# Negated queries and masks: the masked row minimum as the bias of the exponentials

## The chip, the cores and the metric

The kernel runs on one core of one Trainium2 chip. The metric is the device time of one execution in microseconds, as the median over several executions.

## The reference

One layer of a decoder trunk on a sequence of 2048 positions with 1024 features, in float32. The input is normalised and projected; of the projection 512 columns go to eight attention heads of 64 and 2 x 512 columns to a gated linear recurrence (RG-LRU with a short convolution). Both results are joined by an output projection, and a squared-ReLU MLP of width 4096 follows, each with norms and residual.

The attention is a mixture of three dilated sliding windows (window 128 with dilation 1, 512 with 4, 2048 with 16). For each branch:

```python
s = einsum('bchnqd,bchnkd->bchnqk', qb, kb) * (HEAD_DIM ** -0.5)
s = where(valid, s, -inf)
mx = max(s, axis=-1, keepdims=True)
p = exp(s - mx)
den = sum(p, axis=-1)
o = einsum('bchnqk,bchnkd->bchnqd', p, vb) / den[..., None]
lse = mx[..., 0] + log(den)
```

The branches' outputs are then weighted by the softmax over their `lse`.

## The kernel before

All products run as three passes over operands that are split in a high and a low part (`split`, L52: ACT casts the high part at L54, DVE or POOL subtracts it at L55). The sequence is worked in two halves of 1024 positions (`hf` 0 and 1).

First the input projection of both halves runs, with the recurrence and the attention of the first half among it. The order of these steps is the string `ORDER` (L1557), in which `a0` to `a3` are the attention of four pairs of heads, `q..` projections of queries, keys and values (`Project.qkv`, L203) and `r..` blocks of the recurrence (`recurrent_block`, L296). In this part the order of the instructions on each engine is chosen by the framework's scheduler from a simulated timeline (`schedule_with_timeline_sim`, L1610).

Then the first half goes through output projection, MLP input (`mlp_in`) and MLP output (`mlp_out`). PE's order is written by hand from here on. The attention of the second half is interleaved with the first half's `mlp_out` by `interleave` (L1299); in this block ACT, DVE and SP run in the written order too (L1538). `interleave` takes one step of `mlp_out` after another (a product of three matmuls, L1140 to L1142, and a part of the split of a later factor, L1223 on ACT and L1225 on DVE), and puts the parts of an attention unit between them. The exponentials of a unit are issued behind the first of these steps. The second half's projections and MLP follow.

The attention has two parts for each head. Part A (`part_a`, L501) handles the window of dilation 1: per step two blocks of 128 queries against 256 keys each, in one PSUM bank. Part B (`part_b`, L561) covers the other two windows, merged through a mask that holds the logarithm of how often a key counts: per step 384 or 512 keys in the second half, 128 and 256 together in the first. A unit is one (head, block) of part A or one (head, residue) of part B. For each:

- PE writes the scores into PSUM (L529 for A, L586 and L587 for B).
- `softmax_rows` (L400): for each block DVE adds the mask, writes the masked scores to `sm` and their row maximum to one column of the statistics tile `st[:, 0]` (L404: a custom instruction and a read of its accumulator). Then one DVE instruction writes the negated maxima of the step to `neg` (L411). `exps` (L413) has ACT take exp(sm + neg) in place, with the row sums to `st[:, 1]` (L415). In the first half `exps` is called at once; in the second it is returned to `interleave`.
- PE transposes the probabilities (L377), ACT and DVE split them (`thA`, `tlA`, `thB`, `tlB`; L54, L55), PE multiplies them by the values (L553, L612), and `fold` (L394) adds the halves.

`join` (L630) brings the maxima and sums of both parts together: PE lays them out (L644, L646), DVE forms the larger maximum and the differences (L651 to L654), ACT their exponentials (L655, L656), and DVE the weights.

The scale of the scores is in the queries: `qkv` multiplies by 1/8 while it applies the norm (L225). The masks are made on the host by `_constants` (L1567), with 0, a logarithm, or -1e30.

Of the kernel before, what the change touches and what calls it, by code (L numbers as in the profile page):

```python
# [8 lines left out]
F32 = mybir.dt.float32  # L9
F32R = mybir.dt.float32r  # L10
AF = mybir.ActivationFunctionType
ALU = mybir.AluOpType
# [3 lines left out]
P = 128  # L16
# [5 lines left out]
HD = 64  # L22
# [12 lines left out]
NEG = -1.0e30  # L35


def f32(ap):
    return ap.bitcast(F32)
# [12 lines left out]
def split(nc, hi, lo, src, lo_eng=None):  # L52

    return (nc.scalar.copy(out=hi, in_=src),  # L54
            (lo_eng or nc.vector).tensor_tensor(out=lo, in0=src, in1=f32(hi), op=ALU.subtract))  # L55
# [31 lines left out]
class Project:  # L87
# [115 lines left out]
    def qkv(self, hf, pr):  # L203

        nc, p, scr = self.nc, self.p, self.scr
        v, pe = nc.vector, nc.tensor
        last = hf == 0 and pr == NP - 1
        steps = [(k, b) for k in range(3) for b in range(NBH)]
        if last:

            steps = [(0, 0), (0, 1), (1, 0), (2, 0), (1, 1), (2, 1)]
        elif hf and pr == FIRST:

            steps = [(0, 0), (1, 0), (0, 1), (1, 1), (2, 0), (2, 1)]
        ws = {}
        for kind, b in steps:
                ct = 4 * kind + pr
                if kind not in ws:
                    ws[kind] = self.load_w(hf, ct)
                w = ws[kind]  # L220
                cs = slice(b * TB, (b + 1) * TB)
                z = self.product(hf, ct, w, b)
                zn = self.pa.tile([P, TB], F32, tag="t512", bufs=3, name=f"zn{hf}_{ct}_{b}")
                if kind == 0:
                    v.scalar_tensor_tensor(out=zn, in0=z, scalar=HD ** -0.5, in1=self.bc[b], op0=ALU.mult,  # L225
                                           op1=ALU.mult)
                else:
                    v.tensor_tensor(out=zn, in0=z, in1=self.bc[b], op=ALU.mult)
                if kind < 2:
                    zh = self.pa.tile([P, TB], F32R, tag="zh", bufs=1, name=f"zh{hf}_{ct}_{b}")  # L230
                    zl = self.pa.tile([P, TB], F32R, tag="zl", bufs=1, name=f"zl{hf}_{ct}_{b}")
                    self.cst["pool"] = split(nc, zh, zl, zn, lo_eng=self.lo)[1]
                    dst = scr["q" if kind == 0 else "k"][hf][pr]
                    for u in range(2):
                        nc.sync.dma_start(out=f32(dst[u, 0, :, cs]), in_=f32(zh[u * HD:(u + 1) * HD, :]))
                        nc.sync.dma_start(out=f32(dst[u, 1, :, cs]), in_=f32(zl[u * HD:(u + 1) * HD, :]))
                else:
                    pt = self.bank("X", f"vt{hf}_{ct}_{b}")
                    for j in range(TB // P):
                        pe.transpose(pt[:, j * P:(j + 1) * P], zn[:, j * P:(j + 1) * P], self.cst["ident"])  # L240
                    ptv = pt.rearrange("p (n h c) -> p n h c", h=2, c=HD)
                    vs = self.pa.tile([P, TB // P, 2, 2, HD], F32R, tag="vst", bufs=1, name=f"vs{hf}_{ct}_{b}")
                    split(nc, vs[:, :, :, 0, :], vs[:, :, :, 1, :], ptv)
                    nc.sync.dma_start(out=f32(scr["v"][hf][pr][cs, :].rearrange("(n p) c -> p n c", p=P)),
                                      in_=f32(vs.rearrange("p n u a c -> p n (u a c)")))
# [106 lines left out]
def attention(tc, p, bank, cst, scr, hf, mask_a_d, mask_b_d, pj, pw=None, px=None):  # L352
# [7 lines left out]
    v, s, g, pe = nc.vector, nc.scalar, nc.gpsimd, nc.tensor  # L360
# [3 lines left out]
    mask_a = p.tile([P, 2 * P], F32, tag="mask_a", name=f"mask_a{hf}")  # L364
    nc.sync.dma_start(out=mask_a, in_=mask_a_d)
    mask_b = p.tile([P, NX * P], F32, tag="mask_b", name=f"mask_b{hf}")
# [32 lines left out]

    def softmax_rows(st, u, cols, sp, sm, parts, mask, name):  # L400

        neg = p.tile([P, len(parts)], F32, tag="neg", bufs=4, name=f"neg{name}")
        for j, (c0, w) in enumerate(parts):
            v.tensor_tensor_reduce(out=sm[:, c0:c0 + w], in0=sp[:, c0:c0 + w], in1=mask[:, mask.shape[-1] - w:],  # L404
                                   scale=1.0, scalar=-3.0e38, op0=ALU.add, op1=ALU.max,
                                   accum_out=st[:, 0, u, cols[j]:cols[j] + 1])
        if len(parts) == 2 and cols[1] != cols[0] + 1:
            mx = st[:, 0, u, cols[0]:cols[1] + 1:cols[1] - cols[0]]
        else:
            mx = st[:, 0, u, cols[0]:cols[0] + len(parts)]  # L410
        v.tensor_scalar(out=neg, in0=mx, scalar1=-1.0, scalar2=None, op0=ALU.mult)  # L411

        def exps(parts=list(parts)):  # L413
            for j, (c0, w) in enumerate(parts):
                s.activation(out=sm[:, c0:c0 + w], in_=sm[:, c0:c0 + w], func=AF.Exp, bias=neg[:, j:j + 1],  # L415
                             accum_out=st[:, 1, u, cols[j]:cols[j] + 1])

        if hf:
            return exps
        exps()  # L420
# [54 lines left out]
    def units(pr):  # L475
# [25 lines left out]
        def part_a(u, b):  # L501
# [5 lines left out]
            def scores(b2):  # L507
                qs, kh, kl, vb, qa = get()
                ka = runs(kh), runs(kl)
                n0 = 4 * b + 2 * b2  # L510
                sp = bank("S", f"S{n_}_{n0}")
                sm = p.tile([P, TB], F32, tag="sm", bufs=SMB[hf], name=f"sm{n_}_{n0}")
                parts = []
                for j in range(2):
                    n = hf * NQH + n0 + j
                    q = qa[:, (n0 + j) * P:(n0 + j + 1) * P]
                    i, r = divmod(n, 4)
                    w = (2 if n else 1) * P
                    c0 = 2 * P * (j + 1) - w
                    parts.append((c0, w))  # L520
                    dst = sp[:, c0:c0 + w].rearrange("p (n c m) -> p n c m", c=NC, m=MR)
                    for x, t in enumerate((kh, kl)):
                        if r:
                            keys = ka[x][:, i, r - 1:r + 1]
                        elif n:
                            keys = across(t, i)
                        else:
                            keys = ka[x][:, 0, 0:1]
                        pe.matmul(dst, q, keys, start=(x == 0), stop=(x == 1))  # L529
                loc[b2] = sm, parts[0][0]  # L530
                return softmax_rows(env["st"]["A"], u, (n0, n0 + 1), sp, sm, parts, mask_a, f"{n_}_{n0}")
# [93 lines left out]
        def ending():  # L625
            return join(pr, env["st"], env["na"], env["nb"])
# [3 lines left out]
    def join(pr, st, na, nb):  # L630
# [5 lines left out]
        for k, sa in enumerate(sas):  # L636
            v.tensor_tensor(
                out=sa, in1=cst["sel"][:, 0:NC].unsqueeze(1).unsqueeze(1).to_broadcast([P, 4, 4, NC]), op=ALU.mult,
                in0=st["A"][:, k].rearrange("p u (i n) -> p n (u i)", n=4).unsqueeze(3).to_broadcast([P, 4, 4, NC]))
# [8 lines left out]
        mA, dA, mB, dB = [pst[0:R, i * P:(i + 1) * P] for i in range(4)]  # L648
        jt = pj.tile([P, TB], F32, tag="jt", bufs=1, name=f"jt{hf}_{pr}")
        gm, eA, eB, dd = [jt[0:R, i * P:(i + 1) * P] for i in range(4)]  # L650
        v.tensor_copy(out=dd, in_=mA)  # L651
        v.tensor_tensor(out=gm, in0=mB, in1=dd, op=ALU.max)
        v.tensor_tensor(out=eA, in0=dd, in1=gm, op=ALU.subtract)
        v.tensor_tensor(out=eB, in0=mB, in1=gm, op=ALU.subtract)  # L654
        s.activation(out=eA, in_=eA, func=AF.Exp)  # L655
        s.activation(out=eB, in_=eB, func=AF.Exp)  # L656
        yield
        v.tensor_tensor(out=dd, in0=dA, in1=eA, op=ALU.mult)
        v.tensor_tensor(out=gm, in0=dB, in1=eB, op=ALU.mult)
# [907 lines left out]
def _constants():  # L1567
    run = np.arange(P).reshape(MR, NC).T.reshape(-1)
    dist = run[:, None] + P - np.concatenate([run, run + P])[None, :]
    mask_a = np.where((dist >= 0) & (dist <= P), 0.0, NEG).astype(np.float32)  # L1570
    dist = np.arange(P)[:, None] + 3 * P - np.arange(4 * P)[None, :]
    mult = ((dist >= 0) & (dist <= P)) * 1 + ((dist >= 0) & (dist % 4 == 0))
    mask_b = np.where(mult > 0, np.log(np.maximum(mult, 1)), NEG).astype(np.float32)
    i = np.arange(P)[:, None]
    sel = np.concatenate([i // MR == np.arange(NC), i % MR == np.arange(MR)], axis=1).astype(np.float32)
    return np.eye(P, dtype=np.float32), sel, mask_a, mask_b
# [37 lines left out]
```

## Time and profile before

| | |
|---|---|
| median of 3 runs | 2313.2 us (2310.83 to 2317.4) |
| the profiled execution | 2311.64 us |
| its span, first to last instruction | 2309.9 us |
| PE busy | 2184.8 us (95%) |
| DVE busy | 1539.9 us (67%) |
| ACT busy | 1231.3 us (53%) |
| POOL busy | 465.9 us (20%) |
| mean share of the DMA engines, 100 to 560 us and 1100 to 1531 us | 0.57 and 0.72 |

PE is TensorE (matmuls), PEld its weight loads, DVE VectorE, ACT ScalarE, POOL GpSimd, SP the engine that issues most DMAs. Matmuls are pipelined and their ends are modelled, so a busy PE is not PE at its peak. Idle time of an engine that is not the bottleneck costs nothing by itself. The chain of waits follows the last instruction back, at each step to what released it or to the instruction before it on its engine; "issue" is time in which the engine waited for nothing that the profile shows. Names such as `sm`, `smB`, `stA`, `neg` are the program's tiles.

### The profile page before, as it was taken

How to read it: one execution, taken by the hardware profiler on the slowest of the kernel's cores; microseconds unless marked ns; L12 is line 12 of the kernel's file. 1: busy time of each engine (PE TensorE's matmuls, PEld its weight loads, DVE VectorE, ACT ScalarE, POOL GpSimd, SP SyncE). 2: the span in 40 equal slices, each digit the busy share in tenths (PEclk: the TensorE clock that was granted, in tenths of full speed). 3: DMA queues.
4: the chain of work that ended last, by engine and by line, in shares of the span. 5: the costliest groups of instructions: out<-in, count | busy, mean ns of one | idle time of the engine just before them, and what ended most of it. 6: DMA issues, size and time to landing. Idle time of an engine off the chain costs nothing.

```text
span 2309.9 us, 30833 instructions
## 1 busy us (share of the span) xinstructions
PE 2184.8 (95%) x10264; PEld 1776.1 (77%) x10264; DVE 1539.9 (67%) x3060; ACT 1231.3 (53%) x2489; POOL 465.9 (20%) x549
## 2 busy tenths in 40 slices
PE   8989989889999899998999999889999999999998
PEld 6668778667788677786777787667878888788887
DVE  6757575887548877674667677767775656545556
ACT  7646464645334555453656666745454545563542
POOL 5543514563213201011001011113200000000003
PEclk9999999999999999999999999999999999999999
DMA  8364574645754586867777777768454433576665
GB/s 288 99 194 154 166 232 146 180 144 151 255 166 155 195 306 255 302 232 268 248 201 211 220 227 204 220 189 257 147 194 169 164 137 155 208 271 195 192 192 182
DMA packets 217553, 466.16 MB, mean 202 GB/s; under 512 B 22465, under 2 KB 77153, under 8 KB 211121
## 3 DMA queue, kind: packets, MB, share of 16 engines
q1 hardware_dynamic: 188624, 329.52, 45.7%
q0 software_dynamic: 28768, 134.66, 16.5%
q8 instruction: 81, 1.33, 0.2%
q14 instruction: 80, 0.65, 0.1%
HBM read 329.75 MB, written 151.13 MB: 208 GB/s over the span
## 4 chain that ended last, share of the span: by engine, by line
PE 59%; DVE 14%; DMA 9%; ACT 7%; issue 5%; POOL 1%; SPq 0%; DVEq 0%; ACTq 0%; POOLq 0%
PE o L1141 6%; PE o L1140 6%; PE o L1142 6%; PE za L1001 4%; PE za L1002 4%; PE za L1003 4%; PE z L198 3%; PE z L199 3%; PE z L200 3%; PE m L827 2%; PE m L825 2%; PE m L826 2%; PE zc L1001 2%; PE zc L1002 2%; PE zc L1003 2%
## 5 line engine op out<-in xcount | busy, mean ns | idle before, releaser
L198 PE MATMUL z<-hH,wH 128*128 128x512 f32 x640 | 263.6, 412 | 17.6 <-ACT wH L54 7.9
L199 PE MATMUL z<-hL,wH 128*128 128x512 f32 x640 | 259.1, 405 | 0.5 <-DVE hL L173 0.5
L200 PE MATMUL z<-hH,wL 128*128 128x512 f32 x640 | 257.9, 404 | 0.0
L198 PEld LDWEIGHTS z<-hH,wH 128*128 128x128 f32 x640 | 122.6, 192 | 51.2 <-ACT wH L54 8.8
L199 PEld LDWEIGHTS z<-hL,wH 128*128 128x128 f32 x640 | 122.3, 191 | 32.0 <-issue 5.1
L200 PEld LDWEIGHTS z<-hH,wL 128*128 128x128 f32 x640 | 122.5, 191 | 28.5 <-issue 3.4
L415 ACT ACTIVATE smB<-smB,negB 128x128 f32<-128x128 f32 (+3 forms) x128 | 71.4, 559 | 103.0 <-DVE negB L411 102.7
L55 POOL TENSOR_TENSOR wL<-wraw,wH 128x512 fp32r<-128x512 f32 x58 | 84.2, 1464 | 115.7 <-ACT wH L54 109.0
L1006 ACT ACTIVATE sq<-sq 128x512 f32<-128x512 f32 x93 | 58.8, 632 | 84.9 <-DVE sq L1010 84.9
L1066 POOL DMA_DIRECT2D sa<-sq x31 | 16.5, 533 | 402.4 <-ACT sq L1007 401.8
L415 ACT ACTIVATE sm<-sm,neg 128x256 f32<-128x256 f32 (+1 forms) x128 | 63.1, 494 | 55.7 <-DVE neg L411 55.2
L55 DVE TENSOR_TENSOR tlB<-pT_B,thB 128x384 fp32r<-128x384 f32 x96 | 57.4, 598 | 44.2 <-ACT thB L54 41.0
L1007 ACT ACTIVATE sq<-sq 128x512 f32<-128x512 f32 x124 | 76.6, 629 | 2.2
L54 ACT CAST wH<-wraw 128x512 fp32r<-128x512 f32 (+1 forms) x81 | 47.2, 612 | 49.5 <-PE z L199 31.7
L1174 POOL TENSOR_TENSOR y<-y,g4b 128x512 f32<-128x512 f32 x8 | 13.0, 1655 | 261.3 <-ACT junk_y L84 261.3
L1077 DVE TENSOR_TENSOR w2s<-w2s 128x512 f32<-128x512 f32 x64 | 44.1, 689 | 32.1 <-DMA w2s<-in_dram 31.2
L404 DVE CUSTOM_DVE_ANT_0 smB<-SB,mask_b 128x128 f32<-128x128 f32 (+3 forms) x128 | 59.5, 482 | 6.8 <-PE pT_B L377 4.2
L377 PE MATMUL pT_B<-ident,smB 128*128 128x128 f32 x320 | 52.7, 280 | 5.3 <-DVE nb L398 2.2
L54 ACT CAST thB<-pT_B 128x384 fp32r<-128x384 f32 x96 | 48.4, 506 | 16.3 <-PE oB L612 14.2
L55 DVE TENSOR_TENSOR tlA<-pT,thA 128x512 fp32r<-128x512 f32 (+1 forms) x64 | 42.5, 668 | 21.0 <-ACT thA L54 20.7
L1001 PE MATMUL za<-hHT,f_6H 128*128 128x512 f32 x128 | 50.6, 396 | 5.2 <-ACT sq L1040 5.1
L1002 PE MATMUL za<-hLT,f_5H 128*128 128x512 f32 x128 | 51.0, 399 | 4.4 <-DVE hLT L55 4.4
(568 smaller groups left out, 7105.7 us busy)
## 6 DMA issues: line engine op xcount, KB each, us to landing
sa<-as POOLq DMA_DIRECT2D x32, 1024.0 KB, 6.5
w1r<-in_dram SPq DMA_DIRECT2D x58, 512.0 KB, 3.8
sa<-sq POOLq DMA_DIRECT2D x31, 768.0 KB, 3.9
wraw<-in_dram SPq DMA_DIRECT2D x79, 256.0 KB, 3.5
w2s<-in_dram SPq DMA_DIRECT2D x16, 1024.0 KB, 7.5
sb<-w2s POOLq DMA_DIRECT2D x16, 1024.0 KB, 6.2
kh<-sk SPq DMA_DIRECT2D x24, 512.0 KB, 5.2
kl<-sk SPq DMA_DIRECT2D x24, 512.0 KB, 6.8
```

Source lines behind the costliest of these rows:

```text
L54: return (nc.scalar.copy(out=hi, in_=src), (lo_eng or nc.vector).tensor_tensor(out=lo, in0=src, in1=f32(hi), op=ALU.subtract))
L55: (lo_eng or nc.vector).tensor_tensor(out=lo, in0=src, in1=f32(hi), op=ALU.subtract))
L198: pe.matmul(z, hi[:, k, :], hh, start=(k == 0), stop=False)
L199: pe.matmul(z, hi[:, k, :], hl, start=False, stop=False)
L200: pe.matmul(z, lo[:, k, :], hh, start=False, stop=(k == KT - 1))
L415: s.activation(out=sm[:, c0:c0 + w], in_=sm[:, c0:c0 + w], func=AF.Exp, bias=neg[:, j:j + 1], accum_out=st[:, 1, u, cols[j]:cols[j] + 1])
L1001: pe.matmul(o, hi[:, k], bh[:, k], start=start and k == 0, stop=False, skip_group_check=True)
L1002: pe.matmul(o, hi[:, k], bl[:, k], start=False, stop=False, skip_group_check=True)
L1003: pe.matmul(o, lo[:, k], bh[:, k], start=False, stop=k == KH - 1, skip_group_check=True)
L1140: pe.matmul(o, ah[:, ts], bh, start=fresh and j == 0, stop=False, skip_group_check=True)
L1141: pe.matmul(o, ah[:, ts], bl, start=False, stop=False, skip_group_check=True)
L1142: pe.matmul(o, al[:, ts], bh, start=False, stop=j == NJ - 1, skip_group_check=True)
```

## The change

The queries are multiplied by -1/8 in place of 1/8, and both masks change sign, so that the masked scores have the opposite sign. The reduction takes their minimum, which is the negative of the former maximum, and stands in `st[:, 0]`. The exponentials have a scale of -1 and take their bias from that column directly; the tile `neg` and the DVE instruction that wrote it are gone. `join` compares by minimum and takes exponentials with a scale of -1.

```diff
@@ qkv
-                    v.scalar_tensor_tensor(out=zn, in0=z, scalar=HD ** -0.5, in1=self.bc[b], op0=ALU.mult,
+                    v.scalar_tensor_tensor(out=zn, in0=z, scalar=-(HD ** -0.5), in1=self.bc[b], op0=ALU.mult,
                                            op1=ALU.mult)
@@ softmax_rows
-        neg = p.tile([P, len(parts)], F32, tag="neg", bufs=4, name=f"neg{name}")
         for j, (c0, w) in enumerate(parts):
             v.tensor_tensor_reduce(out=sm[:, c0:c0 + w], in0=sp[:, c0:c0 + w], in1=mask[:, mask.shape[-1] - w:],
-                                   scale=1.0, scalar=-3.0e38, op0=ALU.add, op1=ALU.max,
+                                   scale=1.0, scalar=3.0e38, op0=ALU.add, op1=ALU.min,
                                    accum_out=st[:, 0, u, cols[j]:cols[j] + 1])
-        if len(parts) == 2 and cols[1] != cols[0] + 1:
-            mx = st[:, 0, u, cols[0]:cols[1] + 1:cols[1] - cols[0]]
-        else:
-            mx = st[:, 0, u, cols[0]:cols[0] + len(parts)]
-        v.tensor_scalar(out=neg, in0=mx, scalar1=-1.0, scalar2=None, op0=ALU.mult)
-
-        def exps(parts=list(parts)):
+
+        def exps(parts=list(parts), cols=list(cols)):
             for j, (c0, w) in enumerate(parts):
-                s.activation(out=sm[:, c0:c0 + w], in_=sm[:, c0:c0 + w], func=AF.Exp, bias=neg[:, j:j + 1],
+                s.activation(out=sm[:, c0:c0 + w], in_=sm[:, c0:c0 + w], func=AF.Exp, scale=-1.0,
+                             bias=st[:, 0, u, cols[j]:cols[j] + 1],
                              accum_out=st[:, 1, u, cols[j]:cols[j] + 1])
@@ join
-        v.tensor_tensor(out=gm, in0=mB, in1=dd, op=ALU.max)
+        v.tensor_tensor(out=gm, in0=mB, in1=dd, op=ALU.min)
         v.tensor_tensor(out=eA, in0=dd, in1=gm, op=ALU.subtract)
         v.tensor_tensor(out=eB, in0=mB, in1=gm, op=ALU.subtract)
-        s.activation(out=eA, in_=eA, func=AF.Exp)
-        s.activation(out=eB, in_=eB, func=AF.Exp)
+        s.activation(out=eA, in_=eA, func=AF.Exp, scale=-1.0)
+        s.activation(out=eB, in_=eB, func=AF.Exp, scale=-1.0)
@@ _constants
-    mask_a = np.where((dist >= 0) & (dist <= P), 0.0, NEG).astype(np.float32)
+    mask_a = -np.where((dist >= 0) & (dist <= P), 0.0, NEG).astype(np.float32)
-    mask_b = np.where(mult > 0, np.log(np.maximum(mult, 1)), NEG).astype(np.float32)
+    mask_b = -np.where(mult > 0, np.log(np.maximum(mult, 1)), NEG).astype(np.float32)
```

## Rows read from the trace of the kernel before

**Rows 1.** Busy time by stretch: us, then each engine's busy us (instructions), clock, DMA, GB/s

```profile
100.00:560.00 460.00, 421.08 (x2115) 338.23 (x2116) 323.41 (x716) 249.71 (x552) 196.75 (x189) 0.96 0.57 172
...
1100.00:1531.00 431.00, 404.81 (x2206) 336.53 (x2204) 308.17 (x766) 274.77 (x617) 37.84 (x68) 1.00 0.72 211
```

**Rows 2.** Groups by form, 1100 to 1531 us: busy us, mean ns | idle before, releaser

```profile
L404 DVE CUSTOM_DVE_ANT_0 sm<-S,mask_a 128x256 f32<-128x256 f32 x64 | 24.3, 416 | 0.1
L415 ACT ACTIVATE smB<-smB,negB 128x512 f32<-128x512 f32 x32 | 23.2, 725 | 42.2 <-DVE negB L411 41.9
...
L411 DVE TENSOR_SCALAR negB<-stB 128x1 f32<-128x1 f32 x64 | 9.8, 154 | 2.2
...
L411 DVE TENSOR_SCALAR neg<-stA 128x2 f32<-128x2 f32 x32 | 5.4, 169 | 1.1
```

**Rows 3.** Waits, 1100 to 1531 us: us in total, times, longest

```profile
ACT smB L415 <- DVE negB L411: 78.2, 54, 3.7
...
ACT sm L415 <- DVE neg L411: 38.8, 27, 2.1
```

**Rows 4.** Chain of waits, 1100 to 1531 us: start us, us, what

```profile
1176.98 0.16 DVE negB L411
...
1263.55 0.34 DVE sm L404
...
1263.93 0.18 DVE neg L411
...
1264.13 1.09 ACT sm L415 x3
...
1519.41 0.04 DVE negB L411
```

**Rows 5.** Busy time by stretch of the second stage, columns as in rows 1

```profile
1123.00:1172.00 49.00, 49.00 (x278) 42.33 (x277) 34.61 (x90) 32.31 (x75) 0.00 (x0) 1.00 0.63 194
1198.00:1230.00 32.00, 29.55 (x177) 24.46 (x177) 23.13 (x64) 22.29 (x53) 0.90 (x2) 1.00 0.51 154
1246.00:1283.00 37.00, 35.65 (x196) 29.81 (x195) 27.24 (x69) 23.42 (x56) 1.12 (x2) 1.00 0.69 220
1303.00:1330.00 27.00, 24.47 (x148) 19.95 (x146) 18.23 (x52) 16.59 (x41) 0.00 (x0) 1.00 0.53 163
1345.00:1386.00 41.00, 40.70 (x225) 34.45 (x223) 30.59 (x77) 28.05 (x65) 1.12 (x2) 1.00 0.73 234
1403.00:1435.00 32.00, 29.28 (x175) 24.30 (x176) 22.74 (x65) 20.31 (x49) 0.46 (x1) 1.00 0.50 160
1435.00:1474.00 39.00, 32.34 (x151) 24.75 (x149) 31.48 (x75) 32.08 (x57) 9.24 (x16) 0.96 0.88 243
1474.00:1531.00 57.00, 55.44 (x303) 46.43 (x303) 41.72 (x99) 34.37 (x79) 2.54 (x4) 1.00 0.53 158
```

**Rows 6.** Groups by form, 100 to 560 us, columns as in rows 2

```profile
L411 DVE TENSOR_SCALAR negB<-stB 128x2 f32<-128x2 f32 x32 | 10.5, 328 | 0.2
...
L318 ACT ACTIVATE r<-pr,vec_br 128x512 f32<-128x512 f32 x13 | 8.8, 681 | 15.9 <-PE pr L313 9.6 <-DVE xc L331 6.3
...
L411 DVE TENSOR_SCALAR neg<-stA 128x2 f32<-128x2 f32 x32 | 7.6, 248 | 0.1
```

**Rows 7.** Chain of waits, 100 to 560 us, columns as in rows 4

```profile
140.85 0.07 DVE neg L411
...
211.06 1.10 DVE neg L411
...
449.15 0.98 DVE negB L411
...
540.89 0.09 DVE negB L411
```

**Rows 8.** PE's waits, 100 to 560 us, columns as in rows 3

```profile
PE pi L315 <- ACT r L318: 7.7, 2, 4.8
PE oA L553 <- DVE state L332: 5.5, 1, 5.5
```

## The prediction

> **What bounds the kernel now.** I first cut the span into stages and read each engine's busy time there. The negations exist in two stages only: 100 to 560 us (attention of the first half of the sequence, among projections and recurrence) and 1100 to 1531 us (attention of the second half, interleaved with the second MLP product). In both PE is busiest: 421 of 460 us and 405 of 431 us; DVE has 323 and 308, ACT 250 and 275 [rows 1]. So PE idles 39 and 26 us there, and what takes work off DVE or ACT can give back little more than that.
>
> Then I read, in the second stage, the groups of instructions by form and the waits. A unit of attention goes in one ring: PE writes scores, DVE adds the mask and takes the row maximum (L404), DVE negates it (L411), ACT takes the exponentials with that as bias (L415), PE transposes, ACT and DVE split the transposes, PE multiplies by the values. 96 negations take 15.2 us there [rows 2], and ACT sat idle until one of them came in 81 cases for 117 us [rows 3]. That idle time is no gain in itself: most of it is ACT having nothing to do.
>
> What counts is the chain that ended last. Walked through this stage in pieces of 20 us, the chain of waits holds a negation 49 times, 19 of the kind of part A (two columns) and 30 of part B (one column); the first, the last and one whole passage of part A are shown [rows 4]. Behind a first reduction the passage reads: second reduction 0.34, negation 0.18, then both exponentials, 1.09 us. Between 1246 and 1283, for instance, the chain is such passages one behind the other, and PE only follows; between 1123 and 1172 PE is never idle, 49.00 of 49 us, and no negation lies on the chain [rows 5]. So the stage changes between PE setting the pace and the DVE-ACT ring setting it.
>
> **The change part by part.** *160 negations go*: 64 in the first stage (18.1 us, because there they take 248 and 328 ns each on average [rows 6]) and 96 in the second.
>
> *Second stage.* Here the orders of ACT, DVE, SP and PE are written out by hand, so nothing else moves. On the chain a part-B negation costs 0.16 plus about 0.02 of issue, 0.18. A part-A one costs 0.18 plus 0.02, 0.20; and since each exponential now needs its own reduction only, the first exponential can start before the second reduction of 0.34 us. The second exponential then waits for its own reduction, but that ends 0.34 us after the first one, while the first exponential takes 0.5 us, so the new wait is over before it is reached and what is queued behind it on ACT (the other exponential, then the casts of the MLP factors) isn't held. A part-A passage is thus worth 0.54. Sum: 30 x 0.18 + 19 x 0.54 = 15.7 us.
>
> That is an upper bound, since PE becomes the pace once the ring is shorter. I cap each stretch by PE's idle time in it [rows 5]: 1198 to 1230, 2.16 wanted (3 A, 3 B), 2.45 idle; 1246 to 1283, 3.06 wanted (4 A, 5 B), 1.35 idle; 1303 to 1330, 1.98 (3 A, 2 B), 2.53 idle; 1345 to 1386, 3.06 (4 A, 5 B), 0.30 idle; 1403 to 1435, 2.16 (3 A, 3 B), 2.72 idle; 1435 to 1474, 0.72 (4 B), 6.66 idle; 1474 to 1531, 2.34 (2 A, 7 B), 1.56 idle. One more B negation at 1177 adds 0.18. With the smaller of each pair the sum is 2.16 + 1.35 + 1.98 + 0.30 + 2.16 + 0.72 + 1.56 + 0.18 = 10.4; I take 10.
>
> Idle time of PE may be too strict a cap, because matmul times overlap. In the stretch without a stall the weight loads are busy 42.33 of 49 us, 86%; between 1246 and 1283 they are at 29.81 of 37, 81% [rows 5]. The Trainium skill ("Perfetto Trace Analysis", section "Identifying the Most-Contended Engine") says that matmul busy time is no good measure of how near PE is to its limit, and that the busy share of the weight loads is. By that, with 86% as full, the caps would be 3.7, 2.5, 3.9, 1.1, 3.9, 10.4 and 3.3 us, and the sum for the stage 13 in place of 10.
>
> *First stage.* The chain holds 13 negations there, 3.15 us together; the first, the last and the two long ones are shown [rows 7]. The long ones (1.10 and 0.98 against some 0.17) are a stall of DVE that its next instruction may inherit, so without them I count 3.15 - 2.08 + 0.34 = 1.4; the earlier first exponential adds up to 8 x 0.34 = 2.7, since 8 of the 13 are of part A. That makes 1.4 to 5.9 if the orders stay. They need not stay: in this stage the queues' orders come from the scheduler's simulated timeline, and 64 instructions fewer on DVE shift it. One operation that lands behind the wrong neighbour has shown what it costs: PE waited 5.5 us once for DVE's state copy (L332) and 4.8 us at the longest for a tanh of ACT (L318) [rows 8]. So the bounds for this stage run from a loss of some 15 us (three such stalls more) to a gain of 8 (5.9 and part of a stall that goes). I take a gain of 2, near what the rows on the chain give.
>
> *At nothing:* the sign in the query's scale (L225) and in the masks, which only changes a constant. The exponentials get a scale of -1 in place of 1; a tanh with a scale and a pointer bias takes 681 ns for 512 columns [rows 6] where the exponential of 512 without a scale takes 725 [rows 2], so a scale costs nothing. The reduction by minimum: nothing shows it, I take the 416 ns of the maximum [rows 2]; it could be shorter or longer, and a tenth either way on the 24.3 us of part A in the second stage is 2.4 us. In the join (L652 to L656) only signs change, 8 times. The stages between, 560 to 1100 and after 1531, hold no negation; they move earlier as a whole.
>
> Sum: 10 + 2 = 12 us against the profiled execution's 2311.6, so 2299.6. The median of the runs shown lies 1.6 above that execution, so I predict 2301.
>
> **The rivals.** *PE or the loads cover it* (27 in 100). After each saving PE or the next load comes last, and only stretches with more idle time than wanted pay: half of the 10.4, and nothing in the first stage, about 5 us; 2308. For it: PE is busy 94% of this stage, and two stretches have 1.35 and 0.30 us idle where 3 are wanted. Against it: in four stretches the idle time exceeds what is wanted [rows 5]. The Trainium skill's page named above says to optimize the most contended engine first, and by busy time that is PE, not DVE; this rival is what that rule gives.
>
> *Slower: the first stage's order is drawn anew* (13 in 100). Place: 100 to 560 us. Four more stalls of the mean of 5.5 and 4.8 us cost 20.6; with the 12 gained that is 8.6 us slower, 2322. It decides from a loss of 19 us on, below that the second stage pays for it. For it: this stage already holds 39 us of PE's idle time, made of such single waits. Against it: PE's idle time can also shrink by the same draw, and DVE has 18 us less to do.
>
> *It does not do what it says* (2 in 100): the exponentials and the next reductions share a tile, and if the framework ordered them by tile, each reduction would wait for an exponential of 0.5 us; ten on the chain are 5 us, sixty 30, slower. Against it: ACT writes its sums into that tile already, and DVE idled 0.1 us before all 64 reductions of part A in the second stage [rows 2].
>
> **How the numbers follow.** A measurement can tell some 0.3% here, 7 us: faster means under 2306, slower over 2320. The forecast keeps 58 in 100, the covered case 27, the two slower ones 15 together. The range takes the uncapped 15.7 with the first stage's best 8 at its low end (24 gained, 2289), and at its high end the forecast's 10 with three stalls more (15.4 lost, 2318), which leaves out the slower rivals and a little below.
>
> **What would show it.** Right: no L411; ACT's idle time before L415 now ends on L404; the first exponential of part A starts before the second reduction ends; the stage from the first L415 of the second half to its last gets some 10 us shorter, with PE's idle time there down from 26 to some 16; the part-A passage 0.5 us shorter. Wrong: that stage is as long as before and DMA or PE fill the chain where negations stood (covered); the stage before 560 us got longer by single PE waits of 3 to 6 us (order); reductions that wait for L415 (shared tile).

## The result and the profile after

The changed kernel takes 2290.5 us (median of 6 runs, 2288.9 to 2294.6) where the kernel before took 2315.0 beside it on the same chip: ratio 0.9885, 95% interval 0.9862 to 0.9908. Faster, as forecast, and just inside the low end of the range, but by some 25 us (the ratio makes it 26.6), not 12: about twice the gain that was forecast.

Where the time went is read from three starts that mark off four stages: the last start of the input projection's product (L198; the first stage ends there), the first product of the first half's `mlp_out` (the second half's attention begins beside it), and the last exponential of part B. The view is that of a line's instructions: count, shortest/median/longest ns, first and last start in us. Before:

```profile
L198 PE MATMUL z<-hH,wH x640: 387/394/1414, 5.1 to 649.6; 128*128 128x512 f32 x160
...
L1140 PE MATMUL o<-b_0H,a_0H x56: 387/393/481, 1072.0 to 2261.2; 128*128 128x512 f32 x56
...
L415 ACT ACTIVATE smB<-smB,negB x128: 386/557/728, 184.8 to 1524.1; 128x128 f32<-128x128 f32 x32, 128x256 f32<-128x256 f32 x32, 128x384 f32<-128x384 f32 x32, 128x512 f32<-128x512 f32 x32
```

After, the same three:

```profile
L198 PE MATMUL z<-hH,wH x640: 387/394/1415, 5.2 to 628.3; 128*128 128x512 f32 x160
...
L1135 PE MATMUL o<-b_0H,a_0H x56: 387/393/477, 1057.1 to 2244.2; 128*128 128x512 f32 x56
...
L409 ACT ACTIVATE smB<-smB,stB x128: 384/562/730, 183.6 to 1505.6; 128x128 f32<-128x128 f32 x32, 128x256 f32<-128x256 f32 x32, 128x384 f32<-128x384 f32 x32, 128x512 f32<-128x512 f32 x32
```

| stage (us) | before | after | difference |
|---|---|---|---|
| first stage, to the last L198 | 649.6 | 628.3 | -21.3 |
| middle, to the first product of `mlp_out` | 422.4 | 428.8 | +6.4 |
| second half's attention, to the last part-B exponential | 452.1 | 448.5 | -3.6 |
| rest, to the end of the span | 785.8 | 786.9 | +1.1 |
| span | 2309.9 | 2292.5 | -17.4 |

These are two single executions, which differ by less than the medians do. The first lesson stands in the first line: the forecast's 2 us were 21 in this pair of executions (17 in the means further down). Busy time by stretch after (columns as in rows 1, the second stretch moved to where the work now lies):

```profile
100.00:560.00 460.00, 437.56 (x2237) 355.14 (x2238) 321.31 (x678) 256.09 (x566) 201.16 (x197) 0.97 0.59 178
1080.00:1510.00 430.00, 406.67 (x2200) 342.30 (x2201) 294.71 (x672) 277.61 (x618) 37.85 (x68) 0.98 0.74 216
```

In the first stage PE is busy for 437.6 of 460 us where it was 421.1 [rows 1]: idle time fell from 39 to 22 us. In the second it fell from 26.2 to 23.3 only, and DVE's busy time is 13 us less; the two windows don't begin and end at the same places of their stage, so "The sum" below gives PE's idle time for the same part of it in all executions.

In the second stage the groups by form (columns as in rows 2) are these:

```profile
L403 DVE CUSTOM_DVE_ANT_0 sm<-S,mask_a 128x256 f32<-128x256 f32 x64 | 24.4, 419 | 1.0 <-PE S L524 0.6
...
L409 ACT ACTIVATE smB<-smB,stB 128x512 f32<-128x512 f32 x32 | 23.2, 724 | 33.4 <-DVE stB L403 33.3
```

The minimum costs what the maximum did (419 ns against 416), and the exponential with a scale what it did without (724 against 725). ACT's waits there (columns as in rows 3):

```profile
ACT smB L409 <- DVE stB L403: 64.2, 50, 2.7
ACT sm L409 <- DVE stA L403: 24.3, 24, 1.4
```

They now end on the reduction, and 117 us have become 88.5 [rows 3]. A part-A passage in the timeline (start us, us, what) does what the forecast said of it:

```profile
1249.12 0.42 DVE L403 CUSTOM_DVE_ANT_0 sm<-S,mask_a 128x256 f32<-128x256 f32 x1
...
1249.47 0.42 DVE L403 CUSTOM_DVE_ANT_0 sm<-S,mask_a 128x256 f32<-128x256 f32 x1
1249.59 0.51 ACT L409 ACTIVATE sm<-sm,stA 128x256 f32<-128x256 f32 x1 [0.77 <-DVE stA L403]
...
1250.10 0.49 ACT L409 ACTIVATE sm<-sm,stA 128x256 f32<-128x256 f32 x1
```

The first exponential starts at 1249.59, while the second reduction runs until 1249.89, and the second one needs no wait. And the chain of waits, where it was one DVE-ACT passage behind the other, is in this stretch now PE's own products and then a load (1240 to 1290 us, columns as in rows 4):

```profile
1252.29 0.48 PE S L524 x4
1252.77 0.23 PE o L1135
1253.47 0.89 PE oB L607 x8
1254.36 0.46 PE pT L377 x4
...
1277.74 0.89 PE oB L607 x8
...
1280.16 9.06 DMA a_4L<-sa
```

The whole stage says the same. These are the shares of its chain by line, before (1100 to 1531 us) and after (1080 to 1510):

```profile
by line: issue 6.8%; PE o L1141 6.5%; PE o L1140 6.5%; PE o L1142 6.2%; ACT sm L415 4.3%; DMA a_13L<-sa 3.9%; DMA a_10L<-sa 3.7%; ACT smB L415 3.7%; DVE smB L404 3.7%; DVE tlB L55 3.6%; DVE sm L404 3.0%; ACT fold L397 2.7%; DVE tlA L55 2.7%
```

```profile
by line: PE o L1136 13.5%; PE o L1135 13.5%; PE o L1137 13.1%; PE oB L607 4.7%; DMA b_4L<-sw 4.2%; PE pT_B L377 3.8%; issue 3.6%; PE oA L548 3.1%; PE pT L377 3.0%; DMA a_9L<-sa 2.8%; PE S L524 2.4%; DMA a_13L<-sa 2.3%; DMA a_4L<-sa 2.1%; AC
```

Added up piece by piece (after: 1085 to 1512.5), the reductions, negations and exponentials of the ring (those that write `sm`, `smB`, `neg` and `negB`) fell from 70 us of the chain to 19, PE's products rose from 125 to 261, and loads stayed at about 50 (49 and 54). The trace of e9 below, which keeps its negations, has 65 us of ring and 147 of PE there; that of e1, which has none, 22 and 248.

### The profile page after: what moved, and what is told of

It is laid out like the page before. It is cut to its first block, busy times and chain, and to the rows that moved or that the text cites. A ratio compares the mean times of both kernels' runs of the same rounds, so it can differ in the third digit from the quotient of the medians.

```text
span 2292.5 us, 30706 instructions
## 1 busy us (share of the span) xinstructions
PE 2182.9 (95%) x10264; PEld 1781.9 (78%) x10264; DVE 1507.5 (66%) x2900; ACT 1233.6 (54%) x2489; POOL 461.7 (20%) x549
## 4 chain that ended last, share of the span: by engine, by line
PE 62%; DMA 11%; DVE 9%; issue 7%; ACT 5%; POOL 2%; SPq 0%; DVEq 0%; POOLq 0%; ACTq 0%
PE o L1136 7%; PE o L1135 7%; PE o L1137 7%; PE za L996 3%; PE za L997 3%; PE za L998 3%; PE z L198 3%; PE z L199 3%; PE z L200 3%; PE m L822 2%; PE m L821 2%; PE m L820 2%; DMA w2s<-in_dram 2%; PE zc L996 2%; PE zc L997 2%
## 5 line engine op out<-in xcount | busy, mean ns | idle before, releaser
L198 PE MATMUL z<-hH,wH 128*128 128x512 f32 x640 | 261.0, 408 | 13.8 <-ACT wH L54 6.8
L198 PEld LDWEIGHTS z<-hH,wH 128*128 128x128 f32 x640 | 122.0, 191 | 49.0 <-ACT wH L54 7.1
L409 ACT ACTIVATE smB<-smB,stB 128x128 f32<-128x128 f32 (+3 forms) x128 | 71.6, 560 | 79.4 <-DVE stB L403 79.1
L409 ACT ACTIVATE sm<-sm,stA 128x256 f32<-128x256 f32 (+1 forms) x128 | 63.1, 495 | 29.3 <-DVE stA L403 29.0
L607 PE MATMUL oB<-thB,vb 128*128 128x256 f32 x192 | 48.6, 282 | 10.4 <-ACT thB L54 9.7
```

Source lines behind the costliest of these rows:

```text
L198: pe.matmul(z, hi[:, k, :], hh, start=(k == 0), stop=False)
```

## The experiments

Three theories for the surplus of the first stage. **Work**: 64 instructions fewer on DVE, each off the path. **Place**: the scheduler had put 55 of the 64 negations of the first half not right behind their reduction but behind other DVE instructions, 157 in all, some three for each of the 55, and the exponential waited for that place too. **Order**: with the negations gone the scheduler draws other queues for all engines of the first stage, and the new draw happens to be better.

They can be told apart because the order can be held: the engines' queues of one kernel are recorded, and before scheduling each instruction gets an order-only edge to its neighbour in that record. An instruction that the record doesn't have (a negation, a copy) goes right behind the last reduction that it reads. "Old order" and "new order" are the queues of the kernel before and of the changed one (the code is shortened):

```python
for a, b in zip(queue, queue[1:]):      # queue: one engine's recorded order
    tc.add_manual_dep(b, a.name, DependencyInfo(NoSync, DATA), reason="order")
```

The starts are those of the three lines above (us), the last columns the ratio to the kernel before with its 95% interval; "held" is the order held.

| kernel | held | first stage's end | mlp_out begins | last part-B exp | that stage | ratio | interval |
|---|---|---|---|---|---|---|---|
| before | free | 649.6 | 1072.0 | 1524.1 | 452.1 | 1 | |
| e5 copies | free | 645.5 | 1067.3 | 1523.9 | 456.6 | 0.9983 | 0.9972 to 0.9995 |
| e3 copies moved up | old | 639.0 | 1068.3 | 1524.0 | 455.7 | 0.9976 | 0.9962 to 0.9990 |
| e9 negations moved up | old | 639.0 | 1063.9 | 1518.2 | 454.3 | 0.9969 | 0.9953 to 0.9985 |
| e6 copies, first half | old | 636.4 | 1059.6 | 1505.9 | 446.3 | 0.9921 | 0.9900 to 0.9942 |
| e4 copies, unread | old | 638.0 | 1059.5 | 1505.5 | 446.0 | 0.9935 | 0.9911 to 0.9959 |
| e7 copies, second half | old | 636.8 | 1067.1 | 1521.8 | 454.7 | 0.9950 | 0.9934 to 0.9966 |
| e8 reversed | old | 635.4 | 1060.3 | 1510.1 | 449.8 | 0.9928 | 0.9910 to 0.9946 |
| e1 changed | old | 634.1 | 1058.2 | 1505.8 | 447.6 | 0.9925 | 0.9904 to 0.9946 |
| e11 changed | old | 635.7 | 1059.8 | 1508.7 | 448.9 | 0.9906 | 0.9893 to 0.9920 |
| e14 changed | old | 634.9 | 1065.3 | 1514.5 | 449.2 | 0.9918 | 0.9894 to 0.9941 |
| e2 negations | new | 635.8 | 1058.0 | 1512.5 | 454.5 | 0.9961 | 0.9942 to 0.9979 |
| e10 copies, second half | new | 635.3 | 1058.1 | 1513.3 | 455.2 | 0.9942 | 0.9924 to 0.9961 |
| e16 the same | new | 629.7 | 1057.1 | 1512.0 | 454.9 | 0.9929 | 0.9903 to 0.9955 |
| e12 unread, first half | free | 640.3 | 1065.0 | 1515.5 | 450.5 | 0.9913 | 0.9889 to 0.9936 |
| changed | free | 628.3 | 1057.1 | 1505.6 | 448.5 | 0.9885 | 0.9862 to 0.9908 |
| e13 changed | free | 629.2 | 1054.8 | 1505.6 | 450.8 | 0.9896 | 0.9878 to 0.9914 |
| e15 changed | new | 628.3 | 1051.8 | 1499.4 | 447.6 | 0.9883 | 0.9863 to 0.9903 |
| e17 changed | new | 633.9 | 1060.4 | 1507.9 | 447.5 | 0.9899 | 0.9868 to 0.9929 |

### Each kernel in the other's order

e1, e11 and e14 are the changed kernel in the old order (no edit but the edges). e2 is the kernel before in the new order, with the negations moved up:

```diff
-        v.tensor_scalar(out=neg, in0=mx, scalar1=-1.0, scalar2=None, op0=ALU.mult)
+        EXTRA.add(v.tensor_scalar(out=neg, in0=mx, scalar1=-1.0, scalar2=None, op0=ALU.mult).ins.name)
```

(`EXTRA` names what isn't in the record.)

> The changed kernel, with every engine's instructions held in the order of the kernel before (the negations left out of it). Theory ORDER: the 24 us come in good part from the order that the scheduler drew anew in the first 560 us; then this kernel gains only the 10 to 14 us that my sum gave, about 2302, and its first stage ends (last product of L198) at some 646 us, near the 650 of before. Theory DIRECT: the negations cost more than I counted, at any order; then it gains the whole 24, about 2291, and the first stage ends near 628.

> The kernel before, with every engine's instructions held in the order of the changed kernel and each negation right behind its last reduction. Theory ORDER: it keeps what the new order is worth, 10 to 14 us faster than before, about 2302, with the first stage ended near 632 us. Theory DIRECT: no faster than before, 2315, first stage ended near 650.

Measured: 0.9925 and 0.9961. Both ends of the first stage lie near 635, two thirds of the way from 649.6 to 628.3, where the expectations had named 646 or 628 for the one and 632 or 650 for the other. So the new order is not needed for most of the gain, and the negations can stay and most of the first stage's gain is there all the same: neither work nor order alone, which leaves place.

### Copies in place of the negations

The changed signs, with a copy where the negation was. e3 has it in both halves, moved up, e6 (`if not hf`) and e7 (`if hf`) in one half only, all in the old order. e5 is e3 with the scheduler free:

```diff
+            EXTRA.add(v.tensor_scalar(out=neg, in0=mx, scalar1=1.0, scalar2=None, op0=ALU.mult).ins.name)
...
-                             bias=st[:, 0, u, cols[j]:cols[j] + 1],
+                             bias=neg[:, j:j + 1],
```

> The changed kernel's signs, minima and scales, but a copy on DVE in the place of each negation, and its result as the bias, in the order of before. Both theories: as before, 2315 within 3 us, since signs and scales were taken to cost nothing. A dearer or cheaper reduction by minimum would show as a difference in L404's mean time and in the total.

> The changed kernel's signs, minima and scales with the copies kept as in e3, but the scheduler draws the order: it comes out instruction for instruction as the order of before, in which 55 of the 64 copies of the first half stand behind other DVE instructions, 157 in all; in e3 every copy stands right behind its reduction. Theory PLACE (the 6 us of e3 come from the copies' place in DVE's queue): as before, 2315 within 3 us. Theory SIGNS (they come from signs, minima or scales): as e3, 2309.

> As e1 (order of before), but the first half's attention keeps its 64 copies, right behind their reductions; the second half's 96 are gone. Against e3 this is the second stage alone. If my sum for that stage holds (10 us, capped by PE's idle time), 2299; by the trace of the changed kernel, where that stage was 4 us shorter, 2305. First stage ends near 639 as in e3.

> As e1, but the second half's attention keeps its 96 copies and the first half's 64 are gone. Against e3 this is the first stage alone: by my sum 2 us, 2307; by the ends of the first stage in e3 and e1 (639 and 634 us), 5 us, 2304. With e6 the two gains should add to that of e1 against e3, 12.6.

e5 puts the copies where the scheduler wants them, and it draws the old queues again, instruction for instruction: 0.9983 (0.9972 to 0.9995), first stage 645.5. Signs, masks, minimum and scale thus cost nothing, and may give some 4 us of the whole (1 to 6 by the interval). e3 differs from e5 in the copies' places alone, and its first stage ends at 639.0. e6 and e7 part the halves: without copies in the second half its stage takes 446.3 us (e6), with them 454.7 (e7), and the ratios are 0.9921 and 0.9950.

### The kernel before with its negations moved up

e9 has the old signs, the old order, and only the edit of e2: the purest test of place.

> The kernel before with its own signs and its own order, except that all 160 negations stand right behind their last reduction (55 of the first half's 64 stood behind other DVE instructions, 157 in all). Theory PLACE: the first stage ends near 638 us, as in e3 and e6 (639.0 and 636.4), not near 648 as before and in e5 (649.6 and 645.5), and the total is 5 to 10 us below before. Theory NO PLACE: first stage 646 to 650, total as before within 3 us.

The first stage ends at 639.0, as in e3, and the whole is 7 us shorter (0.9969): some 10 us of the stage by moving 64 small instructions up in one queue. The mechanism is seen in the passage that the forecast had named as a stall [rows 7]. DVE and ACT in the kernel before (timeline):

```profile
209.31 0.08 DVE L404 DVE_READ_ACCUMULATOR2_ANT stA<- 128x1 f32 x1
209.31 0.55 DVE L55 TENSOR_TENSOR tlA<-pT,thA 128x384 fp32r<-128x384 f32 x1
209.78 1.27 DVE L331 TENSOR_TENSOR_SCAN xc<-r,state,i 128x512 f32<-128x512 f32 x1
210.98 1.19 DVE L411 TENSOR_SCALAR neg<-stA 128x2 f32<-128x2 f32 x1
...
212.20 0.51 ACT L415 ACTIVATE sm<-sm,neg 128x256 f32<-128x256 f32 x1 [1.88 <-DVE neg L411]
```

and in e9:

```profile
208.42 0.08 DVE L404 DVE_READ_ACCUMULATOR2_ANT stA<- 128x1 f32 x1
208.54 0.17 DVE L411 TENSOR_SCALAR neg<-stA 128x2 f32<-128x2 f32 x1
208.61 0.55 DVE L55 TENSOR_TENSOR tlA<-pT,thA 128x384 fp32r<-128x384 f32 x1
209.08 2.27 DVE L331 TENSOR_TENSOR_SCAN xc<-r,state,i 128x512 f32<-128x512 f32 x1
...
209.32 0.51 ACT L415 ACTIVATE sm<-sm,neg 128x256 f32<-128x256 f32 x1
...
211.27 1.23 DVE L637 TENSOR_TENSOR sa<-stA,sel 128x64 f32<-128x64 f32 x1
```

The row maxima stood ready at 209.39, and the exponential started at 212.20: 2.8 us later, behind a split's subtraction, a scan and a long negation. In e9 it started 0.8 us after the last reduction's read ended (208.50 to 209.32). The stall itself didn't go: the scan and `sa` take 2.27 and 1.23 us now, where their medians over the whole execution are 1.28 and 0.22. In this passage DVE's next instructions inherit the stall, as the forecast assumed; what the move saves is the wait for the place in the queue. ACT's idle time that a negation ended, 130 to 560 us (columns as in rows 3), in the kernel before:

```profile
ACT smB L415 <- DVE negB L411: 23.3, 15, 6.7
...
ACT sm L415 <- DVE neg L411: 16.4, 9, 4.5
...
ACT L415 <- DVE negB L411: 4.7, 1, 4.7
```

in e9:

```profile
ACT smB L415 <- DVE negB L411: 17.4, 11, 3.9
...
ACT sm L415 <- DVE neg L411: 7.2, 7, 2.7
...
ACT L415 <- DVE negB L411: 4.9, 1, 4.9
```

and in e11, where no negation is left and the order is the old one:

```profile
ACT smB L409 <- DVE stB L403: 14.1, 10, 3.4
...
ACT sm L409 <- DVE stA L403: 5.4, 5, 2.4
```

44 us, 30 and 20: some three fifths of what goes, goes by the move. The copies show the same, 50 us where the scheduler places them (e5) and 29 moved up (e3). PE's busy time between 100 and 560 us follows, 421.1 in the kernel before [rows 1], then e9:

```profile
100.00:560.00 460.00, 429.61 (x2165) 347.10 (x2166) 338.15 (x728) 254.68 (x563) 198.61 (x191) 0.97 0.58 174
```

and e11:

```profile
100.00:560.00 460.00, 430.45 (x2181) 348.29 (x2182) 322.68 (x667) 255.19 (x564) 197.88 (x192) 0.97 0.58 176
```

This number varies between executions, though: e5, with the queues of the kernel before, had 427.9.

### Copies that nobody reads

e4 has e3's copies, but the bias comes from the statistics tile, so DVE does their work and nobody waits for it. e12 has such copies in the first half only, with the scheduler free.

> As the changed kernel in the order of before, but DVE still makes the copies, which nobody reads: the wait is gone, the work stays. If what the negation costs is its place in the chain (the exponentials wait for it), this gains most of what the changed kernel gains in the old order. If it is DVE's time, it gains little: in the second stage the part-A passage would still start its exponential 0.54 us earlier, but DVE's next instruction would start no earlier; I expect two thirds of the gain of the first run here.

> The changed kernel with 64 copies in the first half that nobody reads, in an order that the scheduler draws anew (it differs from both the old and the new order). It shows how much a draw alone moves the first stage: e4, with unread copies in the old order, ended it at 638.0; I expect 626 to 640 here, and a total of 2290 to 2302. An end far outside 628 to 638 would say that the changed kernel's own order is an ordinary draw; an end of 628 that the old order was a poor one.

In the second half e4 takes 446.0 us, as if there were no copies: what the negations cost there was the wait, not DVE's time. In the first stage it looks the other way round: 638.0, as with copies that are read (638.1, mean of e3, e6 and e9), against 635.4 without any. That is a small difference between single executions: e6 with its copies ended at 636.4, e7 without them at 636.8. e12's queues are a third draw. Its first stage ends at 640.3, just outside what was expected, but its ratio is 0.9913, as in the changed kernel with the old order (0.9906 to 0.9925), so from one execution it can't be said whether this draw is a worse one.

### Reductions in reversed order

e8 is e1 with the two reductions of a step exchanged, so that the first exponential waits for both again:

```diff
-        for j, (c0, w) in enumerate(parts):
+        for j, (c0, w) in reversed(list(enumerate(parts))):
```

> As e1, but where a step has two blocks DVE reduces the second block first, so that the first exponential waits for the later of the two reductions, as it did with the negation; the work and the other order stay. This takes away the early start alone, which I put at 19 x 0.34 = 6.5 us on the chain of the second stage before the cap by PE. If it counts, 2299 to 2301; if PE covers it, 2296 as e1.

The second half's stage takes 449.8 us against 448.5 (the mean of the nine executions with neither a negation nor a copy there), the ratio is 0.9928 against 0.9916 (the mean of e1, e11 and e14): the earlier start of the first exponential is worth 1 to 3 us, which this experiment hardly tells from nothing.

### What the new order is worth

e10 is e7's kernel in the new order, e13 the changed kernel again, e15 the same with its own order held. e16 and e17 repeat e10 and e15, since e10's first stage, the same program as the changed kernel's, ended 6 to 7 us later.

> e1 once more, beside e9 and e10 on one chip, since its runs spread from 2291 to 2303 and the sum of e6 and e7 against e3 (18.7 us) was larger than e1's (12.6). If the parts add, 2291 to 2295 here; if what the first stage gives is lost again later, 2297 to 2300. First stage ends at 634 to 637.

> The changed kernel in its own order, but the second half's attention keeps 96 copies, so it differs from e7 by the order alone. If the new order is worth 7 us in the first stage, that stage ends near 628 (e7: 636.8), and the total is near 2299, 7 to 8 above the changed kernel for the second stage's copies. If the order is worth nothing, first stage 635 and total 2307 as e7.

> The changed kernel itself, beside e14 on the same chip. If the new order is worth 7 us, 7 below e14 and the first stage ends near 628; if it is worth 2 or less, within 3 us of e14 and the first stage ends near 635.

> The changed kernel in the order of before, as e1 and e11 (2296 and 2294): 2294 to 2296, first stage ended at 634 to 637, whatever the new order is worth.

> The changed kernel with its own order written down in the same way as the old one in e14, so instruction for instruction the changed kernel: as e13, a second profile of it, and a check that writing an order down changes nothing by itself.

> The kernel of the run with copies in the second half and the new order, once more. Up to the second half its program is the changed kernel's, and yet its first stage ended at 635.3 us where the changed kernel's three executions ended at 628.3 to 629.2. If that was this execution's own variation: an end of the first stage near 629, a ratio near 0.992 to 0.993 (the changed kernel's 0.9888 and 8 to 10 us for the copies of the second half). If the new order gives nothing as soon as other instructions stand behind it: again 635, and a ratio of 0.994.

> The changed kernel in its own order, beside the run before on the same chip. If the first stage's end of 628 to 629 is the new order's: again 628 to 629, and a ratio of 0.988 to 0.990. If it was luck of three executions: 632 to 636.

e16 ended at 629.7 and e17 at 633.9: e10 was an execution's own variation, and the three ends near 628 were partly luck. Over six executions the new order ends the first stage at 630.8 in the mean (628.3 to 635.3), the old one over five without copies there at 635.4 (634.1 to 636.8): 4.6 us. The ratios of the changed kernel in the two orders lie apart, 0.9906 to 0.9925 (e1, e11, e14) and 0.9883 to 0.9899 (changed, e13, e15, e17): 0.0026 between the means, 6 us. Their single intervals overlap; beside each other on one chip e14 took 2298.6 us, e13 2292.6 and e15 2289.6. Holding the order costs nothing that shows here (e15 held, e13 free). The old order has no such pair: the kernel before was not run with its queues held and its negations in place, and e5, which draws the same queues, stands for it.

### The sum

| step | first stage's end (us) | ratio | us of the whole |
|---|---|---|---|
| as the scheduler placed them (before, e5) | 647.6 | 1 (before) | |
| moved up (e3, e9; stage also e6) | 638.1 | 0.9973 | -6 |
| gone, old order (e1, e11, e14; stage also e7, e8) | 635.4 | 0.9916 | -13 |
| new order (changed, e13, e15, e17; stage also e10, e16) | 630.8 | 0.9891 | -6 |

The stage of the second half's attention takes 454.8 us in the mean of the eight executions with negations or read copies there and 448.5 of the nine without (e4 and e8 left out): 6 us. In the ratios the copies of the second half cost 8 (e7 against e1, e11, e14) to 13 us (e3 against e6), in the new order 10 (e10, e16 against the changed kernel). PE's idle time in this stage, read in all executions from 28 us behind the first product of `mlp_out` to 7 us behind the last exponential, is 25.1 to 29.4 us in those eight (mean 27.0) and 20.9 to 24.5 in those nine (22.4). In the first stage, 100 to 560 us, it is 38.9 and 32.1 as the scheduler placed them, 29.4 to 30.4 moved up, 26.4 to 29.6 without them in the old order, and 22.1 to 27.6 in the new one.

Two things stay open. Place is plain in the stage's end, 9.5 us, but its worth in the whole is not settled: e9 differs from the kernel before by place alone and is 7 us faster (its interval excludes 1), e3 differs from e5 by place alone and gives 2, with intervals that overlap. Up to 4 of the first 6 us in the table may belong to the signs. And the second half's copies cost more in the whole than the stage's end shows; where the rest arises was not found.

## Why the prediction was right or wrong

*The sign of the result, and what was costed at nothing*: right. Scale, masks and minimum cost nothing in the rows (419 and 724 ns) nor in e5, which was not slower but 1 to 6 us faster.

*Second stage, 10 us*: right in mechanism and about in size, 6 by the stage's ends, 8 to 13 in the whole. The cap by PE's idle time was needed: uncapped it was 15.7, and the chain after shows PE's products where the ring stood. The Trainium skill's measure ("Perfetto Trace Analysis", section "Identifying the Most-Contended Engine"), the busy share of the weight loads, had given an estimate of 13, with 86% as full. The weight loads are busy 342.3 of 430 us after, 80%, so for part of the stage something else set the pace. By the stage's ends the idle time came nearer; the whole, 8 to 13, doesn't decide between the two. Inside the term one piece was too large: the early first exponential, 19 x 0.34 = 6.5 before the cap, gave 1 to 3 (e8), which is hardly told from nothing.

*First stage, "I take a gain of 2"*: this step failed; the executions show some 17 (647.6 to 630.8). Two things were missing in it. It priced a negation as its own piece on the chain, 3.15 us for 13 of them (1.4 with the stalls taken off), and not the instructions that stood between the reduction and the negation in DVE's queue. Those lie on the chain under their own names, so the groups and the chain don't charge them to L411; the view of rows 3, read in the first stage, would have (44 us of ACT's idle time ended by a negation, the longest 6.7, where the instruction takes 0.25 to 0.33). The place is worth 9.5 of the 17. And it saw that the order would be drawn anew, but priced that almost only as a loss: 15 us at the high end of the range and four stalls in a rival, against 2 us ("part of a stall that goes") at the low end and nothing in the forecast. The new draw gave 4.6; that it was a better one is luck as far as the forecast goes. The remaining 2.7 are what removal adds once the place is right, inside the 1.4 to 5.9 that the text had "if the orders stay"; that it is DVE's work is argued from e4 and not shown. In the whole, too, removal by itself in a held order makes 13 us, near the 12 forecast; the other half of the gain is place and order.

*The rivals.* Covered by PE or loads: it did cover part, by the stage's ends and PE's idle time more than the cap took in: the loads on the chain stayed at about 50 us, and PE still idles 22 us in the stage. The slower draw: the draw came, and was better; whether it could as well have been worse isn't shown, e12's single execution doesn't settle it. The shared tile: excluded by the passage at 1249.59, where the exponential starts while the next reduction writes the same tile.

*What would show it*: no L411, waits that end on the reduction, the early first exponential all came. PE's idle time in the second stage did not fall from 26 to 16: over the 17 executions above it went from 27.0 to 22.4, with the stage 6 us shorter instead of 10.

## What to carry to other kernels

A small instruction between a producer and a consumer can cost its place in its engine's queue, and not only its duration (here 9.5 us of a stage for 64 of them): ask what stands between it and what it reads, and read the consumer's waits in each stage. Where a scheduler draws the queues, an edit that takes instructions away is three edits (work, place, a new draw), and here they could be told apart because the order was held; the new draw gave 4.6 us that the forecast had not counted, and belongs in a range in both directions. Before removing such an instruction, moving it right behind its producer shows how much was place.

## What was not expected of the hardware

The middle stage, which the edits don't touch, took 421.5 to 430.4 us from one execution to the next, and 423.5 to 428.8 in four executions of the changed kernel. One place accounts for much of it: PE's longest wait for ACT's `sq` there is 4.5 to 5.7 us in the five executions with the longest middle stage (427.4 to 430.4), and at most 3.9 in the twelve of 425 us or less. In e3 PE waits there for ACT (timeline of PE, then of ACT):

```profile
890.58 0.80 PE L1004 MATMUL za<-hHT,f_6H 128*128 128x512 f32 x1 [5.70 <-ACT sq L1043]
```

```profile
889.94 0.59 ACT L1043 COPY sq<-za 128x512 f32<-128x512 f32 x1 [4.64 <-DMA sb<-w2s]
```

In e6, the same two instructions:

```profile
884.71 0.51 PE L1004 MATMUL za<-hHT,f_6H 128*128 128x512 f32 x1 [1.52 <-ACT sq L1043]
```

```profile
884.07 0.58 ACT L1043 COPY sq<-za 128x512 f32<-128x512 f32 x1 [0.47 <-DMA sb<-w2s]
```

In e3 ACT waited 4.64 us for the load, in e6 0.47. It costs more than the wait, for in e3 the granted clock fell too; in e6 it stayed at 1.00. Busy PE by stretch in e3 (us, PE busy, clock, DMA share, GB/s):

```profile
884.00:886.00 2.00, 0.88 (x4) 1.00 0.98 272
886.00:888.00 2.00, 0.00 (x0) 1.00 1.03 432
888.00:890.00 2.00, 0.00 (x0) 0.73 0.99 406
890.00:892.00 2.00, 1.43 (x3) 0.50 1.07 444
892.00:896.00 4.00, 4.00 (x11) 0.53 0.67 281
896.00:900.00 4.00, 4.00 (x19) 1.00 0.37 131
```

During an idle stretch of 5.7 us the clock falls to its lower level of 1.2 GHz (0.50), where it stays until about 896: 11 matmuls run in the 4 us before that and 19 in the 4 us behind it. Why the load comes late in some executions and not in others stays open; it is why stage ends of single executions are compared here stage by stage, and the whole only by ratios of several runs.
